# Moving elementwise sums from GpSimd to VectorE and re-placing work around the weight changes of a hybrid decoder layer

## Chip, cores and metric

One Trainium2 chip, one of its cores. The metric is device time in microseconds (us), from the median of several runs. PE is TensorE, DVE is VectorE, ACT is ScalarE, POOL is GpSimd; SP is the queue from which nearly all transfers are issued.

## What is computed

One layer over 2048 prompt tokens (16 tiles of 128) and 8 x 8 sample tokens (one tile of 64 rows, called the sample). All of it is fp32.

```python
h = rms_norm(x, norm_pre)
z = h @ w_in                                   # 1024 -> 3584 columns
su, sv = gelu(z[..., :o1]), gelu(z[..., o1:o2])
a_out = silu(z[..., o2:o3]) * spatial_gating(su, sv)       # masked 128x128 mixing in chunks
q, k = rotary(rq, pos), rotary(rk, pos) * RET_DK ** -0.5
o, s_final = retention(q, k, rv, s0)           # recurrent state, 4 heads
b_out = silu(rg) * group_norm(o)
x = x + rms_norm(concat([a_out, b_out]) @ w_out, norm_post)
x = x + sigmoid(x @ w_ple_gate) * (p @ w_ple_proj)
```

## The kernel before

Each fp32 operand is split into a high part `hi` and a rest `lo`, and each product is three matmuls (hi·hi, hi·lo, lo·hi). The program is a stream of 128x512 matmuls in a fixed order; a count of these matmuls is its clock (`Stream`, `st.at`, `st.start`). Everything on the other engines is written into the program at a count, each engine runs its own list strictly in that order, and a `yield n` in a helper means "go on n matmuls later". The stages stand one after the other:

- **S** (3 column groups of `w_in`, 17 tiles, 1200 counts): gating part.
- **R0** (17 tiles of 48 counts, the sample 32): the first two retention heads. The sample is ninth of the 17 in it.
- **R1** (8 pairs of tiles of 84 counts, then the sample): the other two heads, with a seven-product (Strassen-like) scheme, `FastR`. It needs sums of quadrants of the weights (`T1` to `T4`, made by `fast_weights`, `combine`) and of pairs of tiles (`S1` to `S4`). The sums of the tiles are made during S and R0 by `spill_sums` and written to memory.
- **C1** (17 tiles): output projection, norm and residual (`c1_post`). The sample is last in it.
- **C2** (8 pairs and the sample, `Fast`): the gate, again with seven products, whose sums of tiles are made by `Fast.total` during C2, and the small projection `p @ w_ple_proj` beside it.

Weights of a stage are made ahead, in the stage before: a load on SP, a sum (line 777) where the scheme wants one, `hi` on ACT (lines 227, 229, 765), `lo` on DVE (lines 236, 238, 770). `fast_fill` sets the counts for the two seven-product stages (28 jobs each, 14 and 18 of them ahead of the last unit of the stage before), `fill` for the others. All big tiles share 101 slots of SBUF. In the retention stages q and k are transposed through memory: POOL makes them (lines 506, 507, 510), DVE transposes (line 191), SP stores four pieces (line 199) and later loads the result (line 519), ACT copies it (line 522), and then PE computes the scores, which DVE masks (line 553). In C1 and C2 ACT copies a product's bank (line 920) before PE adds the next product into that bank.

The parts of the sample's retention that use its stored state begin at `ret["sample", pr]`; `masked_queries` (line 655) and `by_batch` (line 708) are POOL products for it, and `r_sample_state` loads and splits the state.

Of the kernel before, what the change touches and what calls it, by code (L numbers as in the profile page):

```python
# [16 lines left out]
ALU = mybir.AluOpType  # L17
# [5 lines left out]
NT = 16  # L23
# [11 lines left out]
SAMPLE = NT  # L35
# [71 lines left out]
def hybrid_step(ctx: ExitStack, tc: tile.TileContext, a: dict):  # L107
    nc = tc.nc
    V, S, GP, PE, SY = nc.vector, nc.scalar, nc.gpsimd, nc.tensor, nc.sync
# [14 lines left out]
    def slot(label, shape, dt=F32):  # L124

        return ring.tile(shape, dt, tag="slot", name=name(label))
# [7 lines left out]
    def t2k(shape, dt=F32):  # L134
        return slot("t2", shape, dt)
# [7 lines left out]
    def tiny(w):  # L143
        return work.tile([P, w], F32, tag="tiny", name=name("ti"), bufs=16)
# [33 lines left out]
    st = Stream()  # L178
    np_ = lambda t: TS if t == SAMPLE else P

    def store(dst, src, q=None):
        st.later(LAG_D, lambda: (q or SY).dma_start(out=dst, in_=src))
# [62 lines left out]
    def fill(steps, counts):  # L245
        for (load, high, low), c in zip(steps, counts):
            st.at(c - LAG_W, load)
            st.at(c, high)
            st.at(c + 3, low)
# [23 lines left out]
    def load_xT(t):  # L273
        src = a["xsT"] if t == SAMPLE else a["xT"][t]
        raw = xhalves([P, 4, np_(t)])
        for h in range(2):
            SY.dma_start(out=raw[h], in_=src[:, 4 * h : 4 * h + 4, :])
        return raw
# [465 lines left out]
    def fast_weights(src, scale=None):  # L744


        table, raws, jobs = {}, {}, []

        def load(r, c, k):
            raw = slot("wraw", [P, 512])  # L750
            SY.dma_start(out=raw, in_=src(c, 4 * r + k))
            raws[r, c, k] = raw

        def scaled(r, c, k):
            sc = scale and scale(4 * r + k)
            if sc is not None:
                S.mul(out=raws[r, c, k], in_=raws[r, c, k], mul=sc)

        def job(key, k, raw, needs=(), total=None):

            cell = []

            def high():
                hi = slot("W", [P, 512], F32R)
                S.copy(out=hi, in_=raw())  # L765
                cell.append(hi)

            def low():
                lo = slot("W", [P, 512], F32R)
                V.tensor_tensor(out=lo, in0=raw(), in1=f(cell[0]), op=ALU.subtract)  # L770
                table[key, k] = (cell[0], lo)
                cell.clear()

            jobs.append(([lambda n=n: load(*n) for n in needs], [lambda n=n: scaled(*n) for n in needs], total, high, low))

        def combine(dst, x, y, op):
            GP.tensor_tensor(out=raws[dst], in0=raws[x], in1=raws[y], op=op)  # L777

        for k in range(4):
            job("B11", k, lambda k=k: raws[0, 0, k], [(0, 0, k)])  # L780
        for k in range(4):
            job("T1", k, lambda k=k: raws[0, 0, k], [(0, 1, k)],
                lambda k=k: combine((0, 0, k), (0, 1, k), (0, 0, k), ALU.subtract))
        for k in range(4):
            job("T2", k, lambda k=k: raws[0, 0, k], [(1, 1, k)],
                lambda k=k: combine((0, 0, k), (1, 1, k), (0, 0, k), ALU.subtract))
        for k in range(4):
            job("B22", k, lambda k=k: raws[1, 1, k])
        for k in range(4):
            job("T3", k, lambda k=k: raws[0, 1, k], [],  # L790
                lambda k=k: combine((0, 1, k), (1, 1, k), (0, 1, k), ALU.subtract))
        for k in range(4):
            job("T4", k, lambda k=k: raws[0, 0, k], [(1, 0, k)],
                lambda k=k: combine((0, 0, k), (1, 0, k), (0, 0, k), ALU.subtract))
        for k in range(4):
            job("B21", k, lambda k=k: raws[1, 0, k])
        return table, jobs

    def fast_fill(jobs, counts):
        for (loads, scales, total, high, low), c in zip(jobs, counts):  # L800
            for fn in loads:
                st.at(c - 8 - LAG_W, fn)
            for fn in scales:
                st.at(c - 9, fn)
            if total:
                st.at(c - 7, total)
            st.at(c, high)
            st.at(c + 4, low)

    class Fast:  # L810
# [4 lines left out]
        order = ORDER  # L815
# [29 lines left out]

        def total(self, x, y, op):
            out = slot("sum", [P, 4, 4, 32])
            GP.tensor_tensor(out=out, in0=x, in1=y, op=op)  # L848
            return out

        def prep(self):
# [132 lines left out]
    def spill_sums(j):  # L984

        t0, t1 = 2 * j, 2 * j + 1
        r0, r1 = load_xT(t0), load_xT(t1)
        yield 20
        s2 = slot("sum", [P, 4, P])
        todo = [  # L990
            ("S1", r1[1], lambda: GP.tensor_tensor(out=r1[1], in0=r1[0], in1=r1[1], op=ALU.add)),
            ("S2", s2, lambda: GP.tensor_tensor(out=s2, in0=r1[1], in1=r0[0], op=ALU.subtract)),
            ("S4", r0[1], lambda: GP.tensor_tensor(out=r0[1], in0=r0[1], in1=s2, op=ALU.subtract)),
            ("S3", r0[0], lambda: GP.tensor_tensor(out=r0[0], in0=r0[0], in1=r1[0], op=ALU.subtract)),
        ]
        for key, raw, total in todo:
            total()
            yield 10
            hi, lo = slot("A", [P, 4, P], F32R), slot("A", [P, 4, P], F32R)
            S.copy(out=hi, in_=raw)  # L1000
            yield 6
            V.tensor_tensor(out=lo, in0=raw, in1=f(hi), op=ALU.subtract)
            for o, d in zip((hi, lo), xsum[j][key]):
                store(d, f(o))
            yield 20

    class FastR(Fast):

# [54 lines left out]
    def c1_post(t, part, bank):  # L1063
        src = (yield from result_of(t, bank))[0 : np_(t)]
        n = np_(t)
        if part == 0:
            c1["acc", t] = tiny(2)[0:n]
        acc = c1["acc", t]
        c1[part, t] = src
        junk = t2k([P, 512])[0:n]  # L1070
        S.activation(out=junk, in_=src, func=AF.Square, accum_out=acc[:, part : part + 1])  # L1071
        if part == 0:
            return
        yield 5
        r = tiny(1)[0:n]
        GP.tensor_tensor(out=r, in0=acc[:, 0:1], in1=acc[:, 1:2], op=ALU.add)
        rms_scale(r, r, n, 1.0 / D)
        yield 6
        x2 = [h[0:n] for h in c1.pop(("tok", t))]
        for j in range(2):  # L1080
            w = t2k([P, 512])[0:n]
            V.scalar_tensor_tensor(  # L1082
                out=w, in0=c1.pop((j, t)), scalar=r, in1=ret["npost"][j][0:n], op0=ALU.mult, op1=ALU.mult
            )
            yield 3
            GP.tensor_tensor(out=x2[j], in0=x2[j], in1=w, op=ALU.add)  # L1086
            store(x2d[t][:, 512 * j : 512 * j + 512], x2[j])
        yield 12
        bt = blocks(block_rows(n), x2, n)
        scatter(x2T[t], bt, n, S)  # L1090
# [163 lines left out]
    order = list(range(8)) + [SAMPLE] + list(range(8, NT))  # L1254
# [9 lines left out]
    tabR0, stepsR0 = weight_pass(in_specs([3, 4]))  # L1264
    tabR1, jobsR1 = fast_weights(lambda c, k: a["w_in"][6 - c, k], lambda k: npre[:, k : k + 1])
    tabC1, stepsC1 = weight_pass([(g, k, a["w_out"][g, k], retgn[:, k - 4 : k - 3] if k > 3 else None) for g in range(2) for k in range(KD)])
    tabC2, jobsC2 = fast_weights(lambda c, k: a["w_gate"][c, k])
# [1 line left out]

    unitsS = [Unit("S", [0, 1, 2], Remap())] + [Unit("S", [t], Remap()) for t in order[3:]]  # L1270
    unitsS[0].first = True
    unitsR0 = [Unit("R", [t], tabR0, 0) for t in order]
    unitsR1 = [FastR(p, tabR1, 1, RETENTION if j else ORDER) for j, p in enumerate(pairs)] + [FastR([SAMPLE], tabR1, 1, ORDER)]
    unitsC1 = [Unit("C", [t], tabC1) for t in list(range(NT)) + [SAMPLE]]
    unitsC2, before = [], []
    for j, tiles in enumerate(pairs[:4] + [[SAMPLE]] + pairs[4:]):
        aside = [ple_products(*tg) for tg in before]
# [11 lines left out]
    begin, c = {}, 0  # L1289
# [4 lines left out]
    with tc.manual_schedule(engines={ENG.PE, ENG.SP, ENG.Activation, ENG.DVE, ENG.Pool}):  # L1294
# [44 lines left out]
        for j in range(NT // 2):  # L1339
            st.start(spill_sums(j), 350 + 190 * j)  # L1340
        last = begin[unitsR0[-1]]
        fast_fill(jobsR1, [last - 22 * (14 - j) for j in range(14)] + [last + 8 + 8 * j for j in range(14)])
        last = begin[unitsR1[-2]]
        fill(stepsC1, [last + 50 + 5 * j for j in range(16)])
        for pr, u in ((0, unitsR0[8]), (1, unitsC1[4])):
            ret["sample", pr] = begin[u] + (PH_U if pr == 0 else 0)
            st.start(r_sample_state(pr), begin[u] - 96)
        last = begin[unitsC1[-1]]
        fast_fill(jobsC2, [last - 20 * (18 - j) for j in range(18)] + [last + 8 + 9 * j for j in range(10)])
        fill(stepsP, [last + 90 + 10 * j for j in range(4)])  # L1350

        def c1_norm():
# [1 line left out]
            for h in range(2):  # L1354
                SY.dma_start(out=ret["npost"][h], in_=a["npost"][:, 512 * h : 512 * h + 512])

        st.at(begin[unitsC1[0]] + 20, c1_norm)

        def start_prep(u):
            u.prepping = st.start(u.prep())  # L1360
# [125 lines left out]
```

## Time and profile before

| | |
|---|---|
| median of 3 runs | 1155.3 us (1153.91 to 1156.11) |
| profiled execution, its own time | 1157.6 us |
| its span, first to last instruction | 1155.8 us |
| PE busy | 1113.7 us (96%) |
| DVE, POOL, ACT busy | 724.4, 548.9, 447.9 us |
| mean granted PE clock | 0.983 of full |

The profiled execution is one run of its own; its time stands 1.8 us above its span and 2.3 us above the median. PE busy is near the span, so what matters is the time in which PE stands still, and the clock that it is granted.

### The profile page before, as it was taken

How to read it: one execution, taken by the hardware profiler on the slowest of the kernel's cores; microseconds unless marked ns; L12 is line 12 of the kernel's file. 1: busy time of each engine (PE TensorE's matmuls, PEld its weight loads, DVE VectorE, ACT ScalarE, POOL GpSimd, SP SyncE). 2: the span in 40 equal slices, each digit the busy share in tenths (PEclk: the TensorE clock that was granted, in tenths of full speed). 3: DMA queues.
4: the chain of work that ended last, by engine and by line, in shares of the span. 5: the costliest groups of instructions: out<-in, count | busy, mean ns of one | idle time of the engine just before them, and what ended most of it. 6: DMA issues, size and time to landing. Idle time of an engine off the chain costs nothing. (4 is left out here: it accounts for less than half of the span.)

```text
span 1155.8 us, 16077 instructions
## 1 busy us (share of the span) xinstructions
PE 1113.7 (96%) x5124; PEld 916.6 (79%) x5124; DVE 724.4 (63%) x1319; ACT 447.9 (39%) x919; POOL 548.9 (47%) x717
## 2 busy tenths in 40 slices
PE   9999999999999999898999998899999978999997
PEld 7888878888888878687888786687788866888886
DVE  4756585467855757768566566655556586547554
ACT  7644444446322334225232324333133344334331
POOL 5656646664344566855333332546646681112110
PEclk9999999999999999999999998899999988999999
DMA  9623525347375574555667667475777654435422
GB/s 315 199 73 110 185 78 192 123 149 245 114 215 182 170 216 133 156 157 164 177 177 207 195 188 233 128 228 164 229 252 230 194 169 131 146 112 167 134 89 102
DMA packets 196372, 197.41 MB, mean 171 GB/s; under 512 B 35648, under 2 KB 129344, under 8 KB 196288
## 3 DMA queue, kind: packets, MB, share of 16 engines
q1 hardware_dynamic: 186784, 187.74, 51.8%
q10 hardware_dynamic: 9504, 8.65, 2.5%
q8 instruction: 40, 0.66, 0.2%
q14 instruction: 44, 0.36, 0.1%
HBM read 133.80 MB, written 62.52 MB: 170 GB/s over the span
## 5 line engine op out<-in xcount | busy, mean ns | idle before, releaser
L209 PE MATMUL z<-W,A 128*128 128x512 f32 x3752 | 942.2, 398 | 9.0 <-ACT C L920 7.1
L209 PEld LDWEIGHTS z<-W,A 128*128 128x128 f32 x3752 | 704.8, 190 | 153.7 <-ACT C L920 7.5
L209 PE MATMUL s<-W,A 128*128 128x512 f32 x656 | 174.5, 403 | 8.3 <-DVE W L770 4.4
L209 PEld LDWEIGHTS s<-W,A 128*128 128x128 f32 x656 | 123.6, 191 | 34.3 <-DVE W L770 5.7
L209 PEld LDWEIGHTS s<-t,t 128*128 128x128 f32 (+1 forms) x400 | 74.7, 189 | 16.6 <-DVE t L553 3.4
L209 PE MATMUL s<-t,t 128*128 128x128 f32 (+2 forms) x400 | 77.4, 275 | 3.1 <-DVE t L553 3.1
L506 POOL TENSOR_TENSOR t<-t,t 128x256 f32<-128x256 f32 (+1 forms) x34 | 30.1, 886 | 101.2 <-DVE t L503 57.9
L920 ACT COPY C<-z 128x512 f32<-128x512 f32 x64 | 37.5, 586 | 104.5 <-PE z L209 100.0
L191 DVE STREAM_TRANSPOSE t<-t 128x256 f32<-128x256 f32 (+3 forms) x69 | 39.6, 575 | 47.9 <-POOL t L510 32.6
L269 DVE TENSOR_TENSOR A<-X,A 128x512 fp32r<-128x512 f32 (+1 forms) x68 | 49.6, 731 | 30.9 <-ACT A L267 28.5
L267 ACT CAST A<-X 128x512 fp32r<-128x512 f32 (+1 forms) x96 | 57.7, 602 | 27.3 <-DVE bt L191 10.4
L848 POOL TENSOR_TENSOR sum<-X,X 128x512 f32<-128x512 f32 x16 | 23.2, 1448 | 94.3 <-PE z L209 40.5
L770 DVE TENSOR_TENSOR W<-wraw,W 128x512 fp32r<-128x512 f32 x56 | 57.3, 1024 | 16.3 <-ACT W L765 13.6
L569 POOL TENSOR_TENSOR ti<-ti,c_cols 128x2 f32<-128x2 f32 (+1 forms) x34 | 13.5, 397 | 91.6 <-DVE ti L565 91.6
L1086 POOL TENSOR_TENSOR X<-X,t 128x512 f32<-128x512 f32 (+1 forms) x34 | 48.2, 1437 | 12.2 <-DVE t L1082 9.7
L765 ACT CAST W<-wraw 128x512 fp32r<-128x512 f32 x56 | 34.5, 620 | 47.6 <-POOL wraw L777 44.5
L777 POOL TENSOR_TENSOR wraw<-wraw,wraw 128x512 f32<-128x512 f32 x32 | 44.5, 1398 | 8.9 <-DMA wraw<-w_gate 6.1
L1071 ACT ACTIVATE t<-z 128x512 f32<-128x512 f32 x32 | 19.1, 598 | 75.9 <-PE z L209 75.9
L923 DVE TENSOR_TENSOR C<-z,C 128x512 f32<-128x512 f32 x32 | 22.0, 688 | 39.4 <-ACT C L920 24.4
L238 DVE SCALAR_TENSOR_TENSOR W<-W,c_npre,W 128x512 fp32r<-128x512 f32 x40 | 34.0, 878 | 19.1 <-ACT W L229 19.0
L1127 ACT ACTIVATE C<-C 128x512 f32<-128x512 f32 (+1 forms) x34 | 21.5, 632 | 61.4 <-DVE C L923 59.0
L843 DVE TENSOR_TENSOR A<-X,A 128x512 fp32r<-128x512 f32 (+1 forms) x52 | 39.1, 753 | 8.0 <-ACT A L841 7.9
(147 smaller groups left out, 1380.1 us busy)
## 6 DMA issues: line engine op xcount, KB each, us to landing
X<-xT SPq DMA_DIRECT2D x114, 256.0 KB, 3.7
X<-x SPq DMA_DIRECT2D x64, 256.0 KB, 4.2
W<-w_in SPq DMA_DIRECT2D x40, 256.0 KB, 4.9
qkT<-t SPq DMA_DIRECT2D x132, 64.0 KB, 2.6
x2T<-bt ACTq DMA_DIRECT2D x66, 128.0 KB, 3.6
t<-qkT SPq DMA_DIRECT2D x32, 256.0 KB, 3.1
X<-mixT SPq DMA_DIRECT2D x32, 256.0 KB, 4.1
x2d<-X SPq DMA_DIRECT2D x32, 256.0 KB, 2.0
```

Source lines behind the costliest of these rows:

```text
L191: V.transpose(out=by_k[:, k : k + nk], in_=part.rearrange("p (k b r) -> p k b r", b=4, r=32))
L209: PE.matmul(out, lhsT=l, rhs=r, start=start, stop=stop, skip_group_check=again)
L238: V.scalar_tensor_tensor(out=lo, in0=raw, scalar=sc, in1=f(hi), op0=ALU.mult, op1=ALU.subtract)
L267: S.copy(out=hi, in_=r)
L269: eng.tensor_tensor(out=lo, in0=r, in1=f(hi), op=ALU.subtract)
L506: GP.tensor_tensor(out=qk[:, :, 0, :], in0=t1[:, :, 0, :], in1=t2[:, :, 1, :], op=ALU.subtract)
L765: S.copy(out=hi, in_=raw())
L770: V.tensor_tensor(out=lo, in0=raw(), in1=f(cell[0]), op=ALU.subtract)
L777: GP.tensor_tensor(out=raws[dst], in0=raws[x], in1=raws[y], op=op)
L843: V.tensor_tensor(out=lo, in0=raw, in1=f(hi), op=ALU.subtract)
L920: S.copy(out=c[key], in_=banks[b])
L1086: GP.tensor_tensor(out=x2[j], in0=x2[j], in1=w, op=ALU.add)
```

## The change

Four edits. The 130 sums `combine`, `Fast.total`, `spill_sums` and the residual in `c1_post` go from POOL to DVE. The sample's tile goes from ninth to fourth place in R0 and from last to tenth in C1, and its state work of the second heads from C1's fifth unit to its second. Of the seven-product weights 17 instead of 14 jobs (R1) and 21 instead of 18 (C2) are placed ahead of the last unit of the stage before, and 6 of the 16 weights of C1 are made before R1's last pair has begun or early in it. In `spill_sums` the stores stand 10 counts later. The norm weight of C1 is loaded 40 counts earlier.

```diff
         def combine(dst, x, y, op):
-            GP.tensor_tensor(out=raws[dst], in0=raws[x], in1=raws[y], op=op)
+            V.tensor_tensor(out=raws[dst], in0=raws[x], in1=raws[y], op=op)
...
             out = slot("sum", [P, 4, 4, 32])
-            GP.tensor_tensor(out=out, in0=x, in1=y, op=op)
+            V.tensor_tensor(out=out, in0=x, in1=y, op=op)
...
-            ("S1", r1[1], lambda: GP.tensor_tensor(out=r1[1], in0=r1[0], in1=r1[1], op=ALU.add)),
+            ("S1", r1[1], lambda: V.tensor_tensor(out=r1[1], in0=r1[0], in1=r1[1], op=ALU.add)),
...
         for key, raw, total in todo:
             total()
-            yield 10
+            yield 8
             hi, lo = slot("A", [P, 4, P], F32R), slot("A", [P, 4, P], F32R)
             S.copy(out=hi, in_=raw)
-            yield 6
+            yield 8
             V.tensor_tensor(out=lo, in0=raw, in1=f(hi), op=ALU.subtract)
+            yield 10
             for o, d in zip((hi, lo), xsum[j][key]):
                 store(d, f(o))
-            yield 20
+            yield 14
...
-            GP.tensor_tensor(out=x2[j], in0=x2[j], in1=w, op=ALU.add)
+            V.tensor_tensor(out=x2[j], in0=x2[j], in1=w, op=ALU.add)
...
-    unitsR0 = [Unit("R", [t], tabR0, 0) for t in order]
+    unitsR0 = [Unit("R", [t], tabR0, 0) for t in [0, 1, 2, SAMPLE] + list(range(3, NT))]
...
-    unitsC1 = [Unit("C", [t], tabC1) for t in list(range(NT)) + [SAMPLE]]
+    unitsC1 = [Unit("C", [t], tabC1) for t in list(range(9)) + [SAMPLE] + list(range(9, NT))]
...
-        fast_fill(jobsR1, [last - 22 * (14 - j) for j in range(14)] + [last + 8 + 8 * j for j in range(14)])
+        fast_fill(jobsR1, [last - 22 * (17 - j) for j in range(17)] + [last + 8 + 9 * j for j in range(11)])
         last = begin[unitsR1[-2]]
-        fill(stepsC1, [last + 50 + 5 * j for j in range(16)])
-        for pr, u in ((0, unitsR0[8]), (1, unitsC1[4])):
+        fill(stepsC1, [last - 80 + 20 * j for j in range(6)] + [last + 44 + 8 * j for j in range(10)])
+        for pr, u in ((0, unitsR0[3]), (1, unitsC1[1])):
...
         last = begin[unitsC1[-1]]
-        fast_fill(jobsC2, [last - 20 * (18 - j) for j in range(18)] + [last + 8 + 9 * j for j in range(10)])
+        fast_fill(jobsC2, [last - 20 * (21 - j) for j in range(21)] + [last + 8 + 10 * j for j in range(7)])
...
-        st.at(begin[unitsC1[0]] + 20, c1_norm)
+        st.at(begin[unitsC1[0]] - 20, c1_norm)
```

On POOL, at the end of C1 and the beginning of C2, the program had these rows (`wraw` is a quadrant of a weight, `sum` a sum of tiles, `ti` the small factors of the norm; 777, 848 and 1086 are the sums of weights, of tiles and the residual):

```order
L777 TENSOR_TENSOR wraw_9216<-wraw_9402,wraw_9216 128x512
L848 TENSOR_TENSOR sum_9788<-X_9617,X_9619 128x512
L1086 TENSOR_TENSOR X_9687<-X_9687,t_2195_9782 128x512
L1086 TENSOR_TENSOR X_9688<-X_9688,t_2200_9795 128x512
L777 TENSOR_TENSOR wraw_8914<-wraw_9762,wraw_8914 128x512
L777 TENSOR_TENSOR wraw_8961<-wraw_9785,wraw_8961 128x512
L777 TENSOR_TENSOR wraw_8997<-wraw_9819,wraw_8997 128x512
L1076 TENSOR_TENSOR ti_9888<-ti_9822 64x1
L317 TENSOR_SCALAR ti_9888<-ti_9888 64x1
L318 TENSOR_TENSOR ti_9888<-ti_9888,nhalf 64x1
L777 TENSOR_TENSOR wraw_9048<-wraw_9855,wraw_9048 128x512
L1086 TENSOR_TENSOR X_9810<-X_9810,t_2234_9909 64x512
```

In the changed program only the small operations of the norm stand there, three for a tile, and behind them nothing to the end:

```order
L1077 TENSOR_TENSOR ti_9769<-ti_9703 128x1
L317 TENSOR_SCALAR ti_9769<-ti_9769 128x1
L318 TENSOR_TENSOR ti_9769<-ti_9769,nhalf 128x1
L1077 TENSOR_TENSOR ti_9897<-ti_9820 128x1
L317 TENSOR_SCALAR ti_9897<-ti_9897 128x1
L318 TENSOR_TENSOR ti_9897<-ti_9897,nhalf 128x1
```

All of the 128x512 sums are gone from POOL in this place. On DVE the same place of the changed program (`A` is a split tile, `W` a split weight, `bt` the transposed residual; 848, 777 and 1087 are the sums that came over):

```order
L770 TENSOR_TENSOR W_9720<-wraw_8780,W_9710 128x512
L848 TENSOR_TENSOR sum_9735<-X_9653,X_9655 128x512
L843 TENSOR_TENSOR A_9738<-X_9651,A_9737 128x4x4x32
L777 TENSOR_TENSOR wraw_8811<-wraw_9724,wraw_8811 128x512
L848 TENSOR_TENSOR sum_9764<-sum_9735,X_9651 128x512
L843 TENSOR_TENSOR A_9767<-sum_9735,A_9766 128x4x4x32
L777 TENSOR_TENSOR wraw_8862<-wraw_9742,wraw_8862 128x512
L770 TENSOR_TENSOR W_9783<-wraw_8811,W_9775 128x512
L1083 SCALAR_TENSOR_TENSOR t_2203_9785<-z_9638,ti_9769,npost_7878 128x512
L1087 TENSOR_TENSOR X_9692<-X_9692,t_2203_9785 128x512
L1083 SCALAR_TENSOR_TENSOR t_2204_9791<-z_9701,ti_9769,npost_7879 128x512
L848 TENSOR_TENSOR sum_9798<-X_9657,sum_9764 128x512
```

Between the splits (770, 843) that DVE had before there now stand the sums from which they are made, in the order in which they are needed.

On SP, at the end of R1, the load of the transposed q and k of tile 12 (line 519) was preceded by these rows, the stores of the same for tile 13 (`qkT_7559`), of parts of the mixed output (`mixT`) and loads of C1's weights (`w_out`):

```order
L1020 DMA cs_7602<-cs 64x128
L199 DMA qkT_7559<-t_1670_7557 32x4x128
L199 DMA mixT_102<-t_1672_7561 32x4x64
L277 DMA X_7620<-xsT 128x256
L277 DMA X_7621<-xsT 128x256
L199 DMA qkT_7559<-t_1670_7557 32x4x128
L199 DMA mixT_102<-t_1672_7561 32x4x64
L220 DMA W_7632<-w_out 128x512
L199 DMA qkT_7559<-t_1670_7557 32x4x128
L199 DMA mixT_102<-t_1672_7561 32x4x64
L220 DMA W_7646<-w_out 128x512
L519 DMA t_1694_7649<-qkT_7464 128x4x128
```

and in the changed program (there tile 13's is `qkT_7593`, tile 12's `qkT_7490`):

```order
L1021 DMA cs_7638<-cs 64x128
L199 DMA qkT_7593<-t_1687_7591 32x4x128
L199 DMA mixT_102<-t_1689_7595 32x4x64
L220 DMA W_7652<-w_out 128x512
L277 DMA X_7658<-xsT 128x256
L277 DMA X_7659<-xsT 128x256
L199 DMA qkT_7593<-t_1687_7591 32x4x128
L199 DMA mixT_102<-t_1689_7595 32x4x64
L199 DMA qkT_7593<-t_1687_7591 32x4x128
L199 DMA mixT_102<-t_1689_7595 32x4x64
L220 DMA W_7684<-w_out 128x512
L519 DMA t_1713_7687<-qkT_7490 128x4x128
```

From tile 13's first store to tile 12's load there were 14 rows, now there are 13: one load of a weight has gone from between them. Behind this place, the changed program has five loads more for the sample's state and six loads of weights fewer.

## Rows read from the trace of the kernel before

**Rows 1.** The page's first part: busy time (share of the span) xinstructions.

```profile
span 1155.8 us, 16077 instructions
...
PE 1113.7 (96%) x5124; PEld 916.6 (79%) x5124; DVE 724.4 (63%) x1319; ACT 447.9 (39%) x919; POOL 548.9 (47%) x717
```

**Rows 2.** What PE waited for: us in total, times, longest us.

```profile
PE s L209 <- ACT t L522: 14.7, 7, 5.2
PE z L209 <- ACT C L920: 7.1, 1, 7.1
PE s L209 <- DVE W L770: 4.4, 3, 3.5
PE s L209 <- ACT W L227: 3.6, 2, 2.0
```

**Rows 3.** Busy time of the engines in six stretches; PEclk is the granted clock.

```profile
431.00:480.00 49.00, 42.95 (x208) 34.39 (x207) 36.74 (x67) 19.29 (x36) 37.95 (x40) 0.97 0.47 139
539.00:552.00 13.00, 9.50 (x33) 7.59 (x33) 9.89 (x19) 2.90 (x6) 4.51 (x7) 0.74 0.40 111
701.00:717.00 16.00, 10.84 (x40) 8.55 (x39) 8.90 (x15) 7.15 (x14) 2.68 (x4) 0.79 0.93 281
723.00:747.00 24.00, 19.37 (x80) 15.44 (x79) 17.05 (x36) 7.98 (x17) 12.85 (x13) 0.86 0.46 123
929.00:945.00 16.00, 8.94 (x33) 6.94 (x32) 12.11 (x14) 8.58 (x18) 11.98 (x11) 0.79 0.35 104
951.00:972.00 21.00, 16.21 (x54) 11.39 (x53) 12.85 (x19) 9.54 (x18) 5.37 (x4) 0.84 0.44 144
```

**Rows 4.** Timeline of R0 around the sample; idle time before in brackets.

```profile
470.87 2.54 POOL L708 TENSOR_TENSOR W<-W,c_maskb 128x512 fp32r<-128x512 f32 x2
...
471.81 2.16 DVE L1002 TENSOR_TENSOR A<-X,A 128x512 fp32r<-128x512 f32 x1
...
473.89 0.41 DVE L553 TENSOR_TENSOR t<-s,c_mask 128x256 f32<-128x256 f32 x1
...
474.35 0.49 PE L209 MATMUL s<-t,t 128*128 128x128 f32 x2 [3.08 <-DVE t L553]
```

**Rows 5.** Durations by line: ns min/median/max, first and last start.

```profile
L770 DVE TENSOR_TENSOR W<-wraw,W x56: 640/1094/1770, 411.3 to 954.9; 128x512 fp32r<-128x512 f32 x56
L923 DVE TENSOR_TENSOR C<-z,C x32: 659/691/693, 534.0 to 1139.7; 128x512 f32<-128x512 f32 x32
```

**Rows 6.** Timeline at the change from C1 to C2.

```profile
930.93 4.19 POOL L777 TENSOR_TENSOR wraw<-wraw,wraw 128x512 f32<-128x512 f32 x3
...
938.74 0.58 ACT L920 COPY C<-z 128x512 f32<-128x512 f32 x1
...
939.38 10.07 PE L209 MATMUL z<-W,A 128*128 128x512 f32 x36 [7.06 <-ACT C L920]
...
954.91 0.67 DVE L770 TENSOR_TENSOR W<-wraw,W 128x512 fp32r<-128x512 f32 x1
```

**Rows 7.** Timeline of SP and ACT at the end of R1.

```profile
696.13 0.32 SPq L199 DMA_DIRECT2D qkT<-t  x1
...
703.96 0.38 SPq L519 DMA_DIRECT2D t<-qkT  x1
...
707.77 0.62 ACT L522 COPY t<-t 128x512 f32<-128x512 f32 x1 [0.33 <-DMA t<-qkT]
```

**Rows 8.** The chain that ended last, one of its pieces in C2.

```profile
972.18 2.72 PE z L209 x12
```

**Rows 9.** Busy time in 288 to 345 and 345 to 431, their sum.

```profile
sum 143.00, PE 142.47 PEld 119.17 DVE 94.14 ACT 47.45 POOL 69.63; mean PE 71.24 PEld 59.59 DVE 47.07 ACT 23.72 POOL 34.81
```

**Rows 10.** POOL's groups: busy, mean ns, idle before and what ended it.

```profile
L777 POOL TENSOR_TENSOR wraw<-wraw,wraw 128x512 f32<-128x512 f32 x32 | 44.5, 1398 | 8.9 <-DMA wraw<-w_gate 6.1 <-ACT wraw L757 2.7
...
L848 POOL TENSOR_TENSOR sum<-X,X 128x512 f32<-128x512 f32 x16 | 23.2, 1448 | 94.3 <-PE z L209 40.5 <-DVE A L1121 31.5 <-DMA X<-x2T 12.6
...
L991 POOL TENSOR_TENSOR X<-X,X 128x512 f32<-128x512 f32 x8 | 11.0, 1370 | 12.8 <-DMA X<-xT 12.8
```

More of the change, by code (lines that the diff above doesn't have):

```diff
@@ L990, in spill_sums @@
         todo = [
-            ("S1", r1[1], lambda: GP.tensor_tensor(out=r1[1], in0=r1[0], in1=r1[1], op=ALU.add)),
-            ("S2", s2, lambda: GP.tensor_tensor(out=s2, in0=r1[1], in1=r0[0], op=ALU.subtract)),
-            ("S4", r0[1], lambda: GP.tensor_tensor(out=r0[1], in0=r0[1], in1=s2, op=ALU.subtract)),
-            ("S3", r0[0], lambda: GP.tensor_tensor(out=r0[0], in0=r0[0], in1=r1[0], op=ALU.subtract)),
+            ("S1", r1[1], lambda: V.tensor_tensor(out=r1[1], in0=r1[0], in1=r1[1], op=ALU.add)),
+            ("S2", s2, lambda: V.tensor_tensor(out=s2, in0=r1[1], in1=r0[0], op=ALU.subtract)),
+            ("S4", r0[1], lambda: V.tensor_tensor(out=r0[1], in0=r0[1], in1=s2, op=ALU.subtract)),
+            ("S3", r0[0], lambda: V.tensor_tensor(out=r0[0], in0=r0[0], in1=r1[0], op=ALU.subtract)),
         ]
```

## Prediction

> **What bounds the kernel now.** The page's first part says that PE is busy for 1113.7 of 1155.8 us and DVE for 724.4 [rows 1]: 42.1 us of PE's standing still are the first thing to win. The list of PE's waits says for whom: the transposed q and k (line 522), a bank that ACT has not copied (920), weights not yet split (770, 227) [rows 2]. The busy time in stretches then shows where, and that it costs twice: the granted clock falls in them [rows 3]. I count as lost the idle time, plus (1 - clock) x PE busy:
> - R0 beside the sample, 431 to 480: 6.05 + 0.03 x 42.95 = 7.3 us;
> - R0 to R1, 539 to 552: 3.50 + 0.26 x 9.50 = 6.0;
> - R1 to C1, 701 to 717 and 723 to 747: 5.16 + 2.3, and 4.63 + 2.7, together 14.7;
> - C1 to C2, 929 to 945 and 951 to 972: 7.06 + 1.9, and 4.79 + 2.6, together 16.3.
>
> That is 44.3 us in four places; elsewhere PE hardly waits. What ends last in each is read from the timelines. In R0 POOL makes two masks of the sample in 2.54 us; a split on DVE under them takes 2.16, the score mask is queued behind it, and PE waits 3.08 us for that [rows 4]. At C1 to C2 POOL has three sums of weights in a row (4.19 us), ACT's casts need them, the copy of a bank stands behind the casts in ACT's list, and PE waits 7.06 us [rows 6]. At R0 to R1 PE waits for the last split weight [rows 2]. At R1 to C1 it is another thing: SP issues tile 13's first store at 696.13 and, 14 rows later in its list, tile 12's load at 703.96; it lands, and ACT copies at 707.77 while PE stands [rows 7].
>
> **The sums.** 130 go over: 32 of weights, 32 of tiles in S and R0, 32 in C2, 34 of the residual. POOL took 1.40 us for one (4.19 / 3) [rows 6], so it loses about 180 us. On DVE no such sum is in the trace. The nearest row is another subtraction of two 128x512 tiles in SBUF, line 770: 0.64 us at least, 1.09 in the median, 1.77 at most [rows 5]. It took 0.67 us at 954.91, when POOL rested [rows 6]. I take 0.68, since POOL loses just the long partners: 88 us on DVE (83 to 230), so that DVE is busy for some 812 us, 72% of the time.
>
> Line 923 has one input in PSUM and never passes 0.693 us, line 770 with both in SBUF does [rows 5]. The Trainium skill (SBUF — State Buffer, Who interferes with whom) has the rule for it: a DVE instruction with two SBUF inputs contends with a GpSimd instruction that reads SBUF, and the later one waits for the other's end. By that rule 130 sums hold the port 88 us instead of 180; the trace agrees as far as these rows go.
>
> **R0.** The sample's 16 masks for a pair of heads (8 long, 8 short) now run where PE lost 0.53 of 143 us (288 to 431) and POOL was busy for 69.6 [rows 9]. With 16 x 1.27 = 20.3 us at most for these masks [rows 4], and without two pairs' sums (8 x 1.40), POOL comes to 78.7 of 143: room. At the old place masks and sums are both gone from POOL. I keep 1.5 us of the 7.3: gain 5.8 (0 if the wait moves along, 7.3 at best).
>
> **R0 to R1.** Jobs behind the last unit's start fall from 14 to 11, and the last split stands 14 matmuls earlier (count 98 instead of 112). One matmul is 2.72 / 12 = 0.227 us [rows 8], so 3.2 us, against a wait of 3.5 [rows 2]. DVE there gets 11 splits and 7 sums, 18 x 0.68 = 12.2 us, in place of 14 x 1.09 = 15.3. I keep 0.5: gain 5.5 (0 if these take 1.77 us each, 6.0 at best).
>
> **C1 to C2.** In the changed order DVE has 42 instructions from the first split of C1's last tile to the last weight, 96 matmuls before C2 to 24 after: 42 x 0.68 = 28.6 us in 120 x 0.227 = 27.2, 1.4 behind. The last weight is first read 58 matmuls later, 13.2 us, which hides that; the first product's copy must be done within 11 matmuls, 2.5 us, which just hides it. The sample's result and norm no longer stand there. The small projection's weights are tied to the last C1 unit, which is 16 matmuls longer than the sample's: 3.6 us earlier before C2 needs them, as much as PE waited for them (line 227, 3.6) [rows 2]. I keep 3.5 of 16.3 for the copy, which is tight: gain 12.8 (at 1.09 us a row DVE is 18.7 behind, and little is gained; all 16.3 at best).
>
> **R1 to C1.** SP took 7.83 us for 14 rows, 0.56 each [rows 7]; now there are 13, so 0.6 us off a wait of 5.2. Behind it six weights fewer are loaded, but five loads for the sample's state and the two of the norm weight come in, so queue and transfers are as full as before. DVE and ACT lose six weights and get the splits of the state. I take 0 (gain 14.7 if it is cured, loss 5 x 0.56 = 2.8 if the state's loads stand ahead of tile 14's).
>
> Stores of tile sums 10 matmuls later cost nothing: R1 reads them hundreds of matmuls after. Should they be late after all, SP's later loads would be held by 0.56 us a row. C1's sample in the middle is the same work.
>
> **Sum.** 5.8 + 5.5 + 12.8 + 0 = 24.1 us. The profiled execution took 1157.6 us, 1.8 more than its span; less 24.1 it is 1133.5. It lies 2.3 above the median of the runs, so I say 1131.
>
> **Rivals.**
> - *DVE takes POOL's place as what is late.* If sums and splits keep taking 1.09 us, C1 to C2 runs 18.7 - 13.2 = 5.5 us late, about 7.7 with the clock, instead of 16.3, R0 to R1 stays, the sample's 5.8 is won: 14.4, so 1141. For it: DVE is near full in these stretches (12.11 of 16) [rows 3]. Against it: POOL has only small operations left at C1 to C2. The Trainium skill (Perfetto Trace Analysis, Optimizing Scalar/DVE Operations) warns of just this: GpSimd and DVE share a read port, so offloading between the two might not help. By it the sums would win nothing and only the earlier jobs and the moved sample would count, which is this rival; rows 5 show the contention, but also that an addition there is half as long as on POOL.
> - *R1 to C1 is cured too*, because fewer weights load in it: another 14.7, 1116. For it: six loads and splits come earlier. Against: the row count on SP.
> - *Slower: sums on DVE wait for their loads.* POOL stood 12.8, 6.1 and 12.6 us before sums whose tiles had not landed [rows 10]; nothing was queued there that PE needed soon. On DVE, behind a waiting sum stand rotary products, score masks and splits that PE needs. All 31.5 us on PE's path, with 2.3 us of clock for each of four such stops, is 40.7: 1131 + 40.7 = 1172. It decides from 24 us on, if more than 24 of 40.7 reach PE. Against: the 31.5 us lie before 56 sums (32 + 16 + 8), 0.56 us for one, which is less than the 2.5 us that a bank's copy has in hand.
> - *No change*: the waits move to the sample's new places and DVE's list, 1155.
>
> **How the numbers follow.** The forecast 0.60 (its own range 1123 to 1140), DVE late 0.17, cured 0.10, slower 0.08, no change 0.05. The range that leaves out 2 in 10 reaches from the cured case to the lossy bound of DVE's price: 1114 to 1148. A measurement of this kernel tells about 0.2% (2.3 us) from no change. Faster: 0.60 + 0.17 + 0.10 and none of the rest, 0.87; same 0.05; slower 0.08.
>
> **What would show it.** Right: the sums on DVE near 0.68 us; line 770's median below 0.75; no wait for line 920 over 2 us; none for line 553 by the sample's masks; the waits for line 522 at R1 to C1 still there, near 5 and 4 us, with their half clock (0.50 of full, 1.2 GHz). Wrong: DVE idle before sums for loads, with PE's waits behind it; sums above 1 us; a new wait in early R0 or in the middle of C1; or R1 to C1 gone, or grown beyond 18 us.

## The result

The changed kernel takes 1122.5 us (median of 4 runs, 1122.3 to 1123.8) against 1155.6 of the kernel before on the same chip: ratio 0.9719, 95% interval 0.9702 to 0.9735, so 33 us less. Measured a second time it took 1125.2 against 1154.9 (0.9738, 0.9720 to 0.9755): 30 us less. The forecast was 24 us less, 1131, within 1114 to 1148. The profiled execution took 1123.8 us, its span 1122.0.

The page's first part of the changed kernel, answering to [rows 1]:

```profile
PE 1101.2 (98%) x5124; PEld 910.7 (81%) x5124; DVE 762.5 (68%) x1449; ACT 448.5 (40%) x919; POOL 381.1 (34%) x587
```

PE stands still for 20.8 us instead of 42.1, and its busy time fell by 12.5 us with the same 5124 matmuls, while the mean granted clock rose from 0.983 to 0.995 of full. Its waits, answering to [rows 2] (us in total, times, longest):

```profile
PE s L209 <- ACT t L522: 10.9, 7, 4.2
PE z L209 <- DVE C L957: 2.3, 1, 2.3
PE s L1298 <- POOL zero L167: 1.1, 1, 1.1
PE z L209 <- POOL A L1310: 0.4, 1, 0.4
PE z L209 <- DVE W L238: 0.3, 1, 0.3
```

Lines 920, 770, 227 and 553 are gone from the list; what is left is mostly q and k (line 522), and one stop of 2.3 us for line 957 (a sum of the sample's products in R1), which took 0.76 us in the kernel before. The busy time in the stretches that answer to [rows 3], with a new one ahead, 329 to 347:

```profile
329.00:347.00 18.00, 14.88 (x67) 12.22 (x66) 13.67 (x32) 9.57 (x20) 8.02 (x10) 0.91 0.61 186
425.00:480.00 55.00, 55.00 (x275) 46.40 (x274) 44.70 (x98) 25.04 (x47) 25.49 (x32) 1.00 0.67 202
525.00:560.00 35.00, 35.00 (x173) 29.52 (x172) 23.62 (x47) 12.30 (x24) 12.25 (x17) 1.00 0.65 197
690.00:720.00 30.00, 23.50 (x104) 19.22 (x104) 25.28 (x51) 16.47 (x32) 10.04 (x12) 0.89 0.70 212
720.00:745.00 25.00, 24.85 (x122) 20.12 (x121) 17.22 (x43) 9.29 (x24) 11.20 (x19) 1.00 0.65 183
895.00:940.00 45.00, 45.00 (x200) 37.28 (x199) 38.25 (x63) 23.72 (x47) 3.54 (x6) 1.00 0.71 228
```

In the middle of R0, at R0 to R1 and at C1 to C2 nothing is lost any more. Early R0 has a stall that was not there, and at R1 to C1 the first wait of [rows 3] is left and the second is nearly gone. In early R0 the timeline shows:

```profile
328.61 0.69 DVE L991 TENSOR_TENSOR X<-X,X 128x512 f32<-128x512 f32 x1 [6.57 <-DMA X<-xT]
...
328.98 0.39 SPq L635 DMA_DIRECT2D W<-state  x1
...
329.41 0.45 SPq L199 DMA_DIRECT2D qkT<-t  x1
...
329.96 0.38 SPq L635 DMA_DIRECT2D W<-state  x1
...
332.15 0.38 SPq L519 DMA_DIRECT2D t<-qkT  x1
...
335.45 0.62 ACT L522 COPY t<-t 128x512 f32<-128x512 f32 x1
...
336.12 0.79 PE L209 MATMUL s<-t 128*128 128x128 f32 x2 [3.12 <-ACT t L522]
```

Two things stand there that could have caused it: a sum on DVE that waited 6.57 us for its load, and two loads of the sample's state around the last piece of q and k. The experiments e2 and e7 take them one by one.

At R1 to C1 the chain answers to [rows 7]:

```profile
688.62 0.58 SPq L199 DMA_DIRECT2D qkT<-t  x1
...
690.20 0.91 SPq L277 DMA_DIRECT2D X<-xsT  x2
...
691.15 0.43 SPq L199 DMA_DIRECT2D qkT<-t  x1
691.48 1.23 DVE L238 SCALAR_TENSOR_TENSOR W<-W,c_retgn,W 128x512 fp32r<-128x512 f32 x1
691.62 0.43 SPq L199 DMA_DIRECT2D mixT<-t  x1
692.10 0.43 SPq L199 DMA_DIRECT2D qkT<-t  x1
...
693.54 0.43 SPq L519 DMA_DIRECT2D t<-qkT  x1
...
697.40 0.49 PE L209 MATMUL s<-t 128*128 128x128 f32 x2 [4.24 <-ACT t L522]
```

The last pieces of q and k still stand between other rows, and their load is issued 3.9 us before PE goes on. The prices of the sums, in the groups of lines 777, 770 and 923 (ns min/median/max), answer to [rows 5, 10]:

```profile
L777 DVE TENSOR_TENSOR wraw<-wraw,wraw x32: 640/682/1142, 423.5 to 907.9; 128x512 f32<-128x512 f32 x32
...
L770 DVE TENSOR_TENSOR W<-wraw,W x56: 646/682/2560, 402.8 to 919.8; 128x512 fp32r<-128x512 f32 x56
...
L923 DVE TENSOR_TENSOR C<-z,C x32: 674/692/694, 527.9 to 1105.9; 128x512 f32<-128x512 f32 x32
```

### The profile page after: what moved, and what is told of

It reads as the page before. It is cut to its first block, busy times and chain, and to the rows that moved or that the text cites. A ratio compares the mean times of both kernels' runs of the same rounds, so it can differ in the third digit from the quotient of the medians.

```text
span 1122.0 us, 16010 instructions
## 1 busy us (share of the span) xinstructions
PE 1101.2 (98%) x5124; PEld 910.7 (81%) x5124; DVE 762.5 (68%) x1449; ACT 448.5 (40%) x919; POOL 381.1 (34%) x587
## 4 chain that ended last, share of the span: by engine, by line
PE 61%; DMA 2%; DVE 2%; POOL 2%; SPq 1%; issue 1%; ACT 1%; POOLq 0%; DVEq 0%
PE z L209 45%; PE s L209 16%; DMA X<-xT 1%; SPq L199 1%; DMA t<-qkT 1%; POOL t L506 0%; DMA qkT<-t 0%; POOL t L507 0%; DMA A<-xS47l 0%; SPq L1044 0%; DVE C L923 0%; POOL t L510 0%; DVE t L191 0%; POOL ti L570 0%; ACT t L522 0%
## 5 line engine op out<-in xcount | busy, mean ns | idle before, releaser
L209 PE MATMUL s<-W,A 128*128 128x512 f32 x656 | 171.0, 399 | 0.0
L209 PEld LDWEIGHTS s<-t,t 128*128 128x128 f32 (+1 forms) x400 | 74.3, 188 | 13.1 <-issue 2.7
L506 POOL TENSOR_TENSOR t<-t,t 128x256 f32<-128x256 f32 (+1 forms) x34 | 30.6, 900 | 126.2 <-DVE t L503 82.3
L267 ACT CAST A<-X 128x512 fp32r<-128x512 f32 (+1 forms) x96 | 57.7, 602 | 23.8 <-issue 10.6
L269 DVE TENSOR_TENSOR A<-X,A 128x512 fp32r<-128x512 f32 (+1 forms) x68 | 47.0, 693 | 28.1 <-ACT A L267 27.6
L191 DVE STREAM_TRANSPOSE t<-t 128x256 f32<-128x256 f32 (+3 forms) x69 | 39.5, 574 | 36.3 <-POOL t L510 25.6
L1077 POOL TENSOR_TENSOR ti<-ti 128x1 f32<-128x1 f32 (+1 forms) x17 | 4.7, 278 | 125.3 <-ACT t L1072 125.3
L770 DVE TENSOR_TENSOR W<-wraw,W 128x512 fp32r<-128x512 f32 x56 | 42.7, 763 | 5.0 <-ACT W L765 4.6
L238 DVE SCALAR_TENSOR_TENSOR W<-W,c_npre,W 128x512 fp32r<-128x512 f32 x40 | 31.7, 815 | 19.3 <-ACT W L229 19.1
L353 ACT ACTIVATE t<-z,rsall 128x512 f32<-128x512 f32 x29 | 19.9, 688 | 61.7 <-PE z L209 55.0
L269 POOL TENSOR_TENSOR A<-X,A 128x512 fp32r<-128x512 f32 (+1 forms) x28 | 36.2, 1297 | 22.0 <-ACT A L267 21.7
L923 DVE TENSOR_TENSOR C<-z,C 128x512 f32<-128x512 f32 x32 | 22.0, 689 | 30.6 <-ACT C L920 18.2
L843 DVE TENSOR_TENSOR A<-X,A 128x512 fp32r<-128x512 f32 (+1 forms) x52 | 35.9, 690 | 10.1 <-ACT A L841 10.0
```

Source lines behind the costliest of these rows:

```text
L191: V.transpose(out=by_k[:, k : k + nk], in_=part.rearrange("p (k b r) -> p k b r", b=4, r=32))
L209: PE.matmul(out, lhsT=l, rhs=r, start=start, stop=stop, skip_group_check=again)
L238: V.scalar_tensor_tensor(out=lo, in0=raw, scalar=sc, in1=f(hi), op0=ALU.mult, op1=ALU.subtract)
L267: S.copy(out=hi, in_=r)
L269: eng.tensor_tensor(out=lo, in0=r, in1=f(hi), op=ALU.subtract)
L506: GP.tensor_tensor(out=qk[:, :, 0, :], in0=t1[:, :, 0, :], in1=t2[:, :, 1, :], op=ALU.subtract)
```

## The experiments

Three groups of four kernels, each group on one chip with the kernel before beside it (1154.8, 1155.3 and 1154.9 us). The theory after the result: POOL's sums were what came last, as the prediction read C1 to C2. The main rival: the re-placing did it, and the sums matter little.

The table has what PE lost in each stretch of the profiled execution: over windows of 10 us, the idle time plus (1 - clock) x PE busy, added up. The stretches are early R0 (300 to 400), R0's middle (400 to 500), R0 to R1 (520 to 560), R1 (560 to 690), R1 to C1 (690 to 770), C1 to C2 (890 to 990). The ratio is that to the kernel before in the same group.

| kernel | median us | ratio (95%) | early R0 | R0 mid | R0-R1 | R1 | R1-C1 | C1-C2 |
|---|---|---|---|---|---|---|---|---|
| before | 1155.6 | 1 | 0.5 | 7.2 | 5.7 | 2.3 | 15.5 | 16.3 |
| changed | 1122.5 | 0.9719 (0.9702-0.9735) | 4.6 | 0 | 0 | 3.1 | 9.2 | 0 |
| changed again (e11) | 1125.2 | 0.9738 (0.9720-0.9755) | 4.3 | 0 | 0 | 4.7 | 9.2 | 0 |
| e1 sums alone | 1141.7 | 0.9884 (0.9861-0.9906) | 0 | 2.0 | 4.0 | 2.6 | 15.8 | 10.2 |
| e2 all but the sums | 1129.0 | 0.9778 (0.9760-0.9795) | 4.8 | 0.1 | 0 | 4.1 | 11.8 | 2.7 |
| e3 sample back | 1134.5 | 0.9826 (0.9809-0.9844) | 0.9 | 10.8 | 0 | 3.1 | 6.3 | 5.4 |
| e4 jobs back | 1127.7 | 0.9771 (0.9748-0.9795) | 4.7 | 0 | 2.5 | 2.8 | 11.0 | 0.3 |
| e5 C1's weights back | 1125.6 | 0.9738 (0.9722-0.9753) | 4.2 | 0 | 0 | 2.2 | 10.6 | 0 |
| e6 sample alone | 1139.2 | 0.9861 (0.9845-0.9878) | 6.2 | 0 | 5.1 | 1.8 | 12.6 | 3.3 |
| e7 state early | 1125.1 | 0.9731 (0.9708-0.9754) | 2.6 | 0 | 0 | 3.4 | 10.3 | 0 |
| e8 loads on POOL | 1125.2 | 0.9740 (0.9722-0.9758) | 5.1 | 0 | 0 | 5.0 | 12.0 | 0 |
| e9 jobs 16 earlier | 1147.2 | 0.9926 (0.9910-0.9943) | 0 | 10.9 | 4.7 | 2.9 | 11.5 | 9.8 |
| e10 C1's weights alone | 1148.7 | 0.9951 (0.9933-0.9968) | 0.3 | 7.2 | 4.7 | 2.3 | 7.9 | 16.3 |

How far one execution is from the next: e9 has the order of the kernel before until its first moved job, in the middle of C1 (about 770 us); ahead of that it loses 10.9 instead of 7.2 in R0's middle and 11.5 instead of 15.5 at R1 to C1. So a difference under 4 us in one cell proves nothing by itself.

**e1: the sums alone.** In the kernel before:

```diff
-            GP.tensor_tensor(out=raws[dst], in0=raws[x], in1=raws[y], op=op)
+            V.tensor_tensor(out=raws[dst], in0=raws[x], in1=raws[y], op=op)
```

and the same for the other six calls of the change's diff.

> The kernel before with only the 130 sums moved from POOL to DVE; every unit, job and store stands as before. Theory A (POOL's sums were what came last: the weights' sums at C1 to C2, and by contention the splits at R0 to R1 and beside the sample): these three losses, 16.3 + 6.0 + part of 7.3 us, go without any re-placing, so 1130 to 1138 against 1155.6 of before, and no wait for line 920 over 2 us. Theory B (the re-placing did it: sample among other tiles, more weights ahead): 1150 to 1157 here, and the wait for line 920 at C1 to C2 stays near 7 us. Theory C (DVE has no room for the sums without the re-placing): DVE is late instead, 1140 to 1150, with waits for line 770.

13.1 us less, which lies in the third theory's range, but C1 to C2 keeps 10.2 of 16.3 with not one sum left on POOL. PE waits for line 770 at R0 to R1 alone. PE's waits:

```profile
PE s L209 <- ACT t L522: 13.1, 6, 5.3
PE z L209 <- ACT C L920: 3.0, 1, 3.0
PE s L209 <- ACT W L227: 2.9, 2, 1.8
PE s L209 <- DVE W L770: 2.7, 1, 2.7
```

What the copy (line 920) stands behind there, in ACT's timeline:

```profile
924.01 0.63 ACT L1071 ACTIVATE t<-t 64x512 f32<-64x512 f32 x1 [1.10 <-DVE t L312]
...
924.64 0.60 ACT L765 CAST W<-wraw 128x512 fp32r<-128x512 f32 x1
...
925.27 0.58 ACT L920 COPY C<-z 128x512 f32<-128x512 f32 x1
```

It is the sample: line 312 adds up its result on DVE, line 1071 squares it on ACT, and the copy is queued behind. DVE comes late to line 312 because its own list is full here: it is busy for 19.3 of the 20 us from 905 to 925, as POOL was for 19.8 of the 20 us from 915 to 935 in the kernel before. The kernel before has the same just ahead of [rows 6]'s copy, ACT first and then DVE:

```profile
932.25 0.62 ACT L765 CAST W<-wraw 128x512 fp32r<-128x512 f32 x1 [2.78 <-POOL wraw L777]
...
934.29 0.62 ACT L841 CAST A<-X 128x512 fp32r<-128x512 f32 x1
937.49 0.63 ACT L1071 ACTIVATE t<-t 64x512 f32<-64x512 f32 x1 [2.58 <-DVE t L312]
```

```profile
932.90 1.09 DVE L770 TENSOR_TENSOR W<-wraw,W 128x512 fp32r<-128x512 f32 x1 [3.08 <-ACT W L765]
933.91 1.75 DVE L843 TENSOR_TENSOR A<-sum,A 128x512 fp32r<-128x512 f32 x1
935.59 1.29 DVE L191 STREAM_TRANSPOSE bt<-X 128x512 f32<-128x512 f32 x2
936.81 0.64 DVE L312 TENSOR_TENSOR t<-z,t 64x512 f32<-64x512 f32 x1
```

ACT's last stop before the copy was for the sample's sum on DVE, 2.58 us. DVE had worked up to that sum without a stop since 932.90, and had stood there for 3.08 us for ACT's cast of 932.25, which had stood for 2.78 us for the first of POOL's three sums. So POOL's sums and the sample's rows are links of one chain: the prediction saw its first link, and left out DVE's list and the sample's sum between that and the copy.

**e2: all but the sums.** The changed kernel with those seven lines back on POOL.

> The changed kernel with all 130 sums back on POOL, so only the re-placing is left. Theory A: the three sums of weights in a row still hold ACT's casts at C1 to C2, only the loss beside the sample (7.3 us) and some 3 of R0 to R1 go: 1143 to 1150. Theory B: 1120 to 1128, as the whole change. Theory C: about 1135, so that neither half does it alone.

25.8 us less, the larger part, just above the rival's range. 13.1 + 25.8 is more than 33, so the two overlap. The stall in early R0 is there with the sums on POOL (4.8), so the sum that waited on DVE is not its cause. At C1 to C2 2.7 stay, so the second theory is the nearer one.

**e3: the sample back in its old place.**

```diff
-    unitsR0 = [Unit("R", [t], tabR0, 0) for t in [0, 1, 2, SAMPLE] + list(range(3, NT))]
+    unitsR0 = [Unit("R", [t], tabR0, 0) for t in order]
-    unitsC1 = [Unit("C", [t], tabC1) for t in list(range(9)) + [SAMPLE] + list(range(9, NT))]
+    unitsC1 = [Unit("C", [t], tabC1) for t in list(range(NT)) + [SAMPLE]]
-        for pr, u in ((0, unitsR0[3]), (1, unitsC1[1])):
+        for pr, u in ((0, unitsR0[8]), (1, unitsC1[4])):
```

> The changed kernel with the sample's tile back at ninth place in R0 and last in C1 (its state work with it); sums on DVE and jobs ahead stay. Theory A: with POOL's sums gone the sample costs little where it stood, so 1120 to 1127 (the changed kernel is at 1122.5), and perhaps it wins the 3 us of the new stall in early R0. Theory B: the 5.8 us that the prediction gave to the sample's place come back as a loss beside it, 1128 or more, with PE waiting for line 553 or 522 at 460 to 480.

9 to 12 us of the gain go. R0's middle loses 10.8 though POOL has no sum left, C1 to C2 5.4 with the earlier jobs in place; early R0 is back at 0.9. The first theory is refuted here. But the 10.8 are not the price of the sample's place alone: in e1 the sample stands there too, with the sums on DVE, and R0's middle loses 2.0. In e3 the earlier weight jobs come on top; their first sum runs at 416 us, ahead of the sample's masks (from 421 us), in e1 at 432. PE waits for line 522 there, 7.0 us in four stops.

**e4: the jobs back**, 14 and 18 ahead of the last unit.

> The changed kernel with 14 and 18 weight jobs ahead of the last unit again instead of 17 and 21; all else stays. Theory A (sums on DVE suffice): the last split is as late in the list as before, but each row takes 0.68 instead of 1.09 us; at R0 to R1 up to 3 us come back, at C1 to C2 nothing: 1122 to 1126. Theory B (earlier weights did it): C1 to C2 loses its 12.8 us or more again, 1133 to 1140.

R0 to R1 gets 2.5 us back, and PE's list has its wait for line 770 again (2.5); C1 to C2 nothing. The time is some 2.5 us above the changed kernel's second measurement, with intervals that overlap a little, and between the two theories' ranges.

**e5: C1's weights and norm weight back.**

```diff
-        fill(stepsC1, [last - 80 + 20 * j for j in range(6)] + [last + 44 + 8 * j for j in range(10)])
+        fill(stepsC1, [last + 50 + 5 * j for j in range(16)])
-        st.at(begin[unitsC1[0]] - 20, c1_norm)
+        st.at(begin[unitsC1[0]] + 20, c1_norm)
```

> The changed kernel with C1's 16 weights and its norm weight loaded and split where they were before; all else stays. Theory A (the 6 weights made earlier are what shortened R1 to C1, since the queue of SP is then emptier when the last tiles' q and k come back): the second wait for line 522 there, 3.9 us before and 0.15 after, comes back, with its clock, 1126 to 1130. Theory B (the sums on DVE or the place of the sample's state did it): 1121 to 1124, and the wait stays below 1 us.

1125.6, as the changed kernel's second measurement. The second wait at R1 to C1 is 1.4 us: not 3.9, not 0.15. In the changed kernel these weights do not matter.

**e6: the sample alone moved**, e3's diff the other way in the kernel before.

> The kernel before with only the sample's tile moved in R0 and C1, its state work with it; sums on POOL, jobs as before. Theory A (at C1 to C2 the sample's result, norm and residual stood among the weights' sums, and that, not POOL's price for a sum, made the copy of the bank late): of 16.2 us lost there 10 or more go, the 7.2 beside the sample in R0 go, some 4 come in early R0: 1138 to 1145. Theory B (the weights' sums on POOL were late by themselves, as the prediction read it): the wait for line 920 stays at 4 us or more, and the time is 1146 to 1151.

16.1 us less. C1 to C2 falls to 3.3 with all sums on POOL, and the stall in early R0 comes with the sample. PE's waits:

```profile
PE s L209 <- ACT t L522: 14.0, 6, 4.8
PE s L209 <- DVE W L770: 3.6, 1, 3.6
PE z L209 <- DVE C L957: 2.5, 1, 2.5
PE z L209 <- ACT C L920: 1.4, 1, 1.4
```

**e7: the state's loads for R0 earlier.**

```diff
-            st.start(r_sample_state(pr), begin[u] - 96)
+            st.start(r_sample_state(pr), begin[u] - (156 if pr == 0 else 96))
```

> The changed kernel with the loads and splits of the sample's state for R0 begun 60 counts earlier. Theory A (the new stall at 330 to 340, 4.3 us lost with its clock, comes from two state loads that stand in SP's queue ahead of a piece of q and k and of the load behind it): the stall falls below 1 us, 1118 to 1120. Theory B (it comes from the first sum on DVE, which waits 6.6 us for its tile with the rotary products behind it): the stall stays near 3 us, 1121 to 1124.

PE's stop at 336 falls from 3.1 to 1.5 us, and another at 358 grows to 1.2; the time does not differ from the changed kernel's. The state loads are at most a part of the cause, and the rest of it stays open.

**e8: C1's weights loaded from POOL's queue**, `GP.dma_start` for `SY.dma_start` in the loads of `stepsC1`.

> The changed kernel with the 16 loads of C1's weights issued from POOL's queue, not SP's; POOL is idle for two thirds of the time since the sums left it. Theory A (at R1 to C1 it is the rows of SP's queue, 0.56 us each, that hold q and k up): of the 9.0 us lost at 690 to 720 some 4 to 7 go, 1115 to 1119. Theory B (it is the transfers' own time, or the issue on POOL costs POOL as much as it saves SP): 1120 to 1128, with the wait for line 522 still near 4 us.

No gain: the first wait at R1 to C1 is 5.1 us with none of these loads in SP's list. The count of SP's rows alone is not what sets it. The loads landed in 4.0 us in the median, against 4.2 from SP's queue in the changed kernel.

**e9: C2's jobs 16 matmuls earlier, the sample still last**, in the kernel before.

```diff
-        last = begin[unitsC1[-1]]
+        last = begin[unitsC1[-1]] - 16
```

> The kernel before with all weights for C2 and the small projection 16 matmuls (3.6 us) earlier against the beginning of C2, and the sample still last in C1; sums on POOL. This is one half of what moving the sample does there: with a tile of 48 matmuls as the last unit, in place of the sample's 32, all jobs that hang on the last unit stand 16 matmuls earlier before C2. Theory A (this lead is what cures C1 to C2): 16.2 us lost there fall to 5 or less, 1142 to 1147. Theory B (the sample's own rows there, copies, sums and norm, on which ACT waits with a bank's copy behind them, are what was late): 9 us or more stay, 1148 to 1156.

C1 to C2 goes from 16.3 to 9.8, which is what the second theory said; the time, 8 us less, lies between the two theories' ranges. The lead brings about half of what the sample's move brings there (13.0); PE still waits 5.3 us for line 920 and 1.5 for line 1082.

```profile
PE z L209 <- ACT C L920: 5.3, 1, 5.3
...
PE z L209 <- DVE t L1082: 1.5, 1, 1.5
```

**e10: C1's weights alone**, e5's diff the other way in the kernel before.

> The kernel before with only C1's weights (6 of 16 earlier) and its norm weight moved. Theory A (the earlier weights shorten the second wait at R1 to C1): of 3.9 us there 1.5 or less stay, the first stays near 5, and 15.5 us lost become 10 to 12: 1149 to 1152. Theory B (the place of the sample's state and the sums do it): the second wait stays above 3 us, 1153 to 1157.

6.3 us less, R1 to C1 at 7.9. In the timeline PE stops there for 4.4 and then 1.35 us, against 5.2 and 3.9 of before. The second wait is 3.9 us in e1 and e9 too, which have these weights in their old place. So here they do matter, and in e5 they don't.

**e11: the changed kernel again.**

> The changed kernel itself once more, beside the others on one chip: 1121 to 1125, with waits for line 522 near 3 (early R0), 1.5, 1.3, 4.2 us and the last at R1 to C1 between 0.1 and 1.4. Where it comes out near 1125, C1's weights, the early state and the other queue changed nothing that can be told; at 1122 all three cost some 2 to 3 us.

Early weights of C1, early state and the other queue (e5, e7, e8) changed nothing that can be told.

**e12: q and k through POOL's queue.**

```diff
-        scatter(qkT, bt, n)
+        scatter(qkT, bt, n, GP)
-        SY.dma_start(out=raw, in_=qkT.rearrange("a p k r -> p a k r"))
+        GP.dma_start(out=raw, in_=qkT.rearrange("a p k r -> p a k r"))
```

> The changed kernel with the four stores of transposed q and k and the load behind them issued from POOL's queue in place of SP's, in all 34 tiles of the retention. Theory A (what is left at 330 to 340, 640 to 670 and 690 to 720, 16.2 us with its clock, is q and k standing in SP's list behind other loads and stores): two thirds go, 1108 to 1114, and the waits for line 522 fall below 1.5 us. Theory B (it is the way through memory itself, stores' and load's own time): 1118 to 1126. Theory C (POOL, which now waits for DVE's transposes before each store, makes the next q and k later): 1126 or more, and DVE waits longer for POOL at line 191.

1175.4 us, 1.0170 (1.0154 to 1.0186) of the kernel before: PE waits 45.5 us in 14 stops for line 522. The DMA issues (KB, median us to landing):

```profile
qkT<-t POOLq DMA_DIRECT2D x132, 64.0 KB, 2.4
...
t<-qkT POOLq DMA_DIRECT2D x32, 256.0 KB, 4.3
```

against 2.3 and 3.1 from SP's queue in the changed kernel. The stores land as fast, the load takes 1.2 us longer, and each row keeps POOL for 0.56 (stores) or 0.81 us (loads). Theory C's sign and size are right: POOL stood 15.4 us in 8 stops for DVE's transposes before these stores, and DVE's wait for POOL at line 191 rose from 36.2 to 41.4 us (for line 510 it fell from 25.6 to 21.6, for line 580 it rose from 10.6 to 19.8). How the 50 us divide between this and the later landing is not shown. No version was found that beats the changed kernel.

## Why the prediction was right, and which terms were off

The sign, the four places and the double cost of a stop (idle and clock) were right. The six stretches of the table lost 47.5 us before and 16.9 after, 30.6 less, against the sum's 24.1. R1 to C1 and C1 to C2 gave 9.8 us more than forecast, R0 2.7 less; that the misses cancel in part is luck. By its terms:

- **R0, 5.8.** The 7.2 went wholly (1.5 were to stay; the sums alone take the loss to 2.0, e1), but early R0 lost 4.3 to 4.6 instead of 0.5: net some 3. The step that failed is "room" at the new place, which counted POOL's time alone; the load and stores of the sample's q, k and state there were not counted. e6 and e2 have the stall, e3 has not, so it comes with the sample; which of the sample's rows holds PE up is not shown (e7). The prediction had named a new wait in early R0 as a sign of being wrong. The rival that sums on DVE would wait for their loads did occur on DVE, 6.57 us in one place, and cost PE nothing that the same sums on POOL didn't.
- **R0 to R1, 5.5.** 5.7. The jobs do it, as worked out: e2 has no loss there with the sums on POOL; with the old jobs and cheap sums 2.5 stay (e4).
- **C1 to C2, 12.8.** 16.3; the 3.5 kept for the copy was not needed. Here the size was near and the cause was read in part: POOL's sums begin the chain, and the sample's sum ends it (the timelines with e1). With the sums off POOL 10.2 are left (e1), with only the sample moved 3.3 (e6). The prediction named the sample's result and norm as gone, but without a price. And the lead that a longer last unit gives was put down to the small projection only, though `fast_fill` for C2 hangs on the same `last`: e9 shows that this half was worth 6.5.
- **R1 to C1, 0.** 6.3 less by these two profiles, the largest miss, though e9's 11.5 shows that the 15.5 of before was a high one. The step that failed: "queue and transfers are as full as before". The first wait stayed as forecast (4.2; about 5 was said), with a clock of 0.61 in the 4 us from 697 on, so for the most part at 1.2 GHz of 2.4. The second fell from 3.9 to 0.15 (0.23 in e11). C1's earlier weights alone take it to 1.35 (e10); without them the other edits together take it to 1.4 (e5). Either will do; which row of which queue it was stays open. Against this gain a stop grew: line 957's, from 0.76 to 2.3 us. e6 and e2 have it (2.5 and 2.3), e1, e9 and e3 have not (0.8, 0.8, 0.2), so it comes with the sample's move. Two splits of the sample's state (line 644, 0.39 and 0.83 us) stand ahead of it on DVE; the prediction named these splits and gave them no price.
- **The sums' price, 0.68.** Right: 0.682 for line 777. DVE's 812 us were not: it is busy for 762.5. The groups of the 130 sums add up to 91.8 us, 0.71 each in the mean. The durations of DVE's other instructions, added up from the traces, fell from 788.8 to 746.9 us, which the prediction had said of the splits and not put into the total; the rest is overlap of neighbouring rows, which counts once in the busy time.
- **DVE in POOL's place** did not occur in the changed kernel: C1 to C2 loses nothing. In e1, without the re-placing, it did at C1 to C2, though a sum took 0.7 us and not the 1.09 of that rival. The Trainium skill's warning (Perfetto Trace Analysis, Optimizing Scalar/DVE Operations), that moving work between GpSimd and DVE might not help, did not come true here: the sums alone won 1.2% (e1), and 4 to 6.5 us on top of the rest (e2 against both measurements).

One of the tests was worth nothing: line 770's median below 0.75 us. It is 0.693 in e2 too, where the sums are on POOL; the mean would have told (0.98 there, 0.76 here).

## What to carry to other kernels

Where ACT or DVE work through their lists in order, the wait that PE shows has several stops behind it; read the timeline of the engine that releases PE back from the release to its last stop, then that of the engine it stopped for, and so on; every link of this chain is a place for a cure, and the first one found need not be the one that is worth most. Work that hangs on the start of the last unit of a stage moves with that unit's length. Gains of edits that cure links of the same chain don't add: alone, sums, sample and C1's weights won 13, 16 and 6 us, and all edits together 30 to 33.

## What the runs showed of the hardware

The runs show how much DVE's other work shortens once POOL's sums are gone. Groups of DVE (busy us, mean ns) in the kernel before, and in the changed one:

```profile
L770 DVE TENSOR_TENSOR W<-wraw,W 128x512 fp32r<-128x512 f32 x56 | 57.3, 1024 | 16.3 <-ACT W L765 13.6 <-PE z L209 2.2
...
L923 DVE TENSOR_TENSOR C<-z,C 128x512 f32<-128x512 f32 x32 | 22.0, 688 | 39.4 <-ACT C L920 24.4 <-PE z L209 14.3 <-DMA A<-xS43l 0.7
```

```profile
L770 DVE TENSOR_TENSOR W<-wraw,W 128x512 fp32r<-128x512 f32 x56 | 42.7, 763 | 5.0 <-ACT W L765 4.6 <-PE z L209 0.2
...
L923 DVE TENSOR_TENSOR C<-z,C 128x512 f32<-128x512 f32 x32 | 22.0, 689 | 30.6 <-ACT C L920 18.2 <-PE z L209 12.4
```

The subtraction with both inputs in SBUF falls from 1.02 to 0.76 us in the mean (0.79 in e1, where only the sums moved, 0.98 in e2, where all but the sums did), the one with an input in PSUM stays at 0.69. The Trainium skill (SBUF — State Buffer, Who interferes with whom) says that a DVE instruction with two SBUF inputs and a GpSimd one that reads SBUF hold each other up; the traces agree. The load of the transposed q and k landed later from POOL's queue than from SP's, 4.3 against 3.1 us (e12), but the loads of C1's weights did not (4.0 against 4.2 us, e8). The page lists POOL's queue as of another kind, q0 software_dynamic, where SP's is q1 hardware_dynamic, so e8 and e12 change the kind of queue and not only the list in which a row stands.
